# A transformer-and-state-space kernel: its first stage in a new order, with column-grouped modulation products and uniform filter products

## The chip, the cores and the metric

The kernel runs as one program on one NeuronCore of a Trainium2 chip. The metric is the device time of one execution in microseconds (us). The kernel before has a median of 1732.91 us over three runs. The change touches the first stage alone, roughly the first 116 us of the span.

## The reference, cut to what matters

Two blocks follow each other on a sequence of 512 tokens of width 1024, all in float32: an attention layer with a second sequence (`ctx`, 256 tokens) as further keys, a long-convolution ("hyena") layer, two convolutional feed-forwards, then a state-space block. Three pieces of it are computed in the first stage:

```
mod_x = silu(c) @ mod_w[0] + mod_b[0]        # 1024 -> 6*1024; the same for c_ctx
sh1, sc1, ... = split(mod_x, 6)
hx = rmsnorm(x, g) * (1 + sc1) + sh1         # and hc for ctx
kv = hx @ w_dkv                              # first product of the attention layer

# filters of the hyena layer, which need no activations at all
h = sin(freq1 * (z @ w1 + b1)); h = sin(freq2 * (h @ w2 + b2))
h_fwd, h_bwd = split(h @ w3) * exp(-t * |decay|)
filt_f = rfft(concat(h_fwd, 0, reversed h_bwd))
```

## The kernel before, in words

Accurate products of float32 data are made from two rounded parts: `split` writes `hi` (ScalarE) and `lo = x - hi` (VectorE), and `mm3` adds hi*hi, hi*lo and lo*hi. A `Stream` does this for weight blocks of 128x1024: a DMA into a `raw` tile (3 buffers), the `hi` on ScalarE, the `lo` on VectorE (5 buffers each). A float32 product that is not split takes two records on TensorE.

The first stage is written out by hand as a string of tokens, `PLAN`, which `token` works off in order:

- `L` loads and `m` multiplies one of 16 blocks of the modulation weight (128 rows by 1024 columns: 512 of shift, 512 of scale). Blocks 0 to 7 are multiplied in float32 with a stationary operand of 2 columns (`c`, `c_ctx`), blocks 8 to 15 are split first and multiplied with 4 columns. `O` copies the sums out (`scr`), `c` turns them into columns with small products against an identity (`pst`).
- `X` and `C` load tiles of `x` and `ctx`; `q`, `Q` square them and add up; `S`, `T` sum over partitions on TensorE and take 1/rms; `R`, `U` spread that over the partitions on TensorE again; `n`, `N` multiply; `d`, `D` modulate and split.
- `W` loads the three blocks of `w_dkv`; `p` adds one k-step of the three products `psx`, which end the stage's main line.
- `F` advances the generator `hyena_filter` by one `yield`: two steps of the small sine network (`psf`), then for 4 column quarters and 2 signs a `source` (8 products `psh` of 256 columns, then a multiply by the decay window into `ta`), each followed by the `spectrum` of the source before it (16 records `pac`), which is evacuated (`sb`, `ho`) and written to DRAM (`Hd`). `spectrum` has two parts, `q` = 0 and 2, each with its own bank, copy, two adds of 128x256, DMA of 256 KB and `yield`.
- In a `source`, each pair of products uses a stationary tile of 128 rows (`S` whole) and then one of 64 rows (`S[0:64]`).

TensorE's instructions keep the order of the program text (`manual_schedule`). The order on each other queue, SP's list of DMAs among them, is settled at build time by a scheduler with its own idea of when operands are ready, so an entry that it holds to be ready can move ahead of one that stands earlier in the text. Each queue then runs strictly in that order. After the stage come `QPLAN` (four `dq` products, the products of `ctx`) and the attention.

Of the kernel before, what the change touches and what calls it, by code (L numbers as in the profile page):

```python
# [18 lines left out]
L = 512  # L19
# [170 lines left out]
STEPS = "s0 q0 t0 k0 t1 s1 o0 t2 o1 t3 o2 t4 M0 s2 o3 v0 t5 k1 v1 s3 M1 v2 x0 o4 o5"  # L190
PLAN = """F L0 X0 L1 L2 m0 F m1 L3 I9 m2 X1 L4 X6 C4 X3 X7 X4 C0 F X5 X2 q0 L5 V q3 C1 q7 m3 C3 F C5 F m4 L6 L7 q4 L8 q5 q6 L9 m5 F q1 q2 C6 C2 L10 C7 S F R F m6 m7 n3 n0 L11 n6 F n5 L12 n1 O0 m8 m9 F n7 F c0 L13 m10 d1 m11 n2 d0 F L14 F L15 n4 d3 Q0 m12 Q5 F Q7 m13 Q2 m14 m15 d2 O1 F K W0 W1 Q1 c1 W2 d4 F p0 Q4 Q3 F p2 F d7 Q6 T p3 U N0 p1 d5 d6 N3 p6 N7 N1 N2 N6 F p5 N4 D4 D3 D6 N5 p4 F D7 D2 D1 p7 D0 D5 F"""


def build(nc, tc, A, dbg=None):
# [203 lines left out]

    c4 = const.tile([128, 8, 4], F32R, name="c4")
    c2v = c2.rearrange("p (k s) -> p k s", s=2)  # L400
    act.activation(c4[:, :, 0:2], c2v, AF.Copy)
    dve.tensor_tensor(out=c4[:, :, 2:4], in0=c2v, in1=c4[:, :, 0:2].bitcast(F32), op=ALU.subtract)
# [11 lines left out]

    pp = opool(es_a, "pp0", 5, space=PSUM)
    psm = [pp.tile([4, 512], F32, name=f"psm{i}", tag="mm") for i in range(4)]

    def hyena_inputs(hp, t, n1):
        for n, sh, src in (("zT", [33, L], A["zT"]), ("fw1", [33, 64], A["fw1"]), ("fw2", [64, 64], A["fw2"]),
                           ("fv", [64, 4], A["fvec"]), ("fw3", [128, 2048], A["fw3"]), ("nt", [128, 4], A["negt"]),  # L420
                           ("db", [1, 1024], A["dbias"]), ("dec", [128, 1024], A["decay"].broadcast_to([128, 1024])),
                           ("tabs", [128, 1536], A["fwt"]))[len(t):n1]:
            t[n] = hp.tile(sh, F32, name=n)
            nc.sync.dma_start(out=t[n], in_=src)

    def range_sin(tp, out, a, shape, quarter=False, tag=""):

        n = tp.tile(shape, F32, name="rsn" + tag, tag="rsn" + tag if tag else "ho", **({"bufs": 1} if tag else {}))
        if quarter:
# [11 lines left out]
        dve.tensor_scalar(out=r, in0=r, scalar1=PI32, scalar2=-PI32, op0=ALU.min, op1=ALU.max)  # L441
        act.activation(out, r, AF.Sin)

    Hd = dram.tile([2, 8, 128, 512], F32, name="Hd")

    def hyena_filter(hp, tp, pp, t):
        fv = t["fv"]
        src, wgt = t["zT"], t["fw1"]
        for i in range(2):
            ps = pp.tile([128, L], F32, name="psf", tag="mm")  # L450
            pe.matmul(ps[:64], wgt, src, start=True, stop=True)
            a = tp.tile([64, L], F32, name="fa", tag="ho")
# [20 lines left out]
        for i, op in enumerate((ALU.add, ALU.subtract)):  # L473
            w = fw3[:, :1024] if i else hp.tile([128, 1024], F32, name="w3")
            dve.tensor_tensor(out=w, in0=fw3[:, :1024], in1=fw3[:, 1024:], op=op)
            wh = hp.tile([128, 1024], F32R, name=f"w3h{i}", tag=("w3h", "w3")[i])
            wl = hp.tile([64, 1024], F32R, name=f"w3l{i}")
            act.activation(wh, w, AF.Copy)
            dve.tensor_tensor(out=wl, in0=w[0:64], in1=wh[0:64].bitcast(F32), op=ALU.subtract)
            w3.append((wh, wl))  # L480
        W = 256

        def source(qd, ab, win):
            cs = slice(qd * W, qd * W + W)
            ta = []
            for r in range(0, 4, 2):
                ps = pp.tile([128, 2, W], F32, name="psh", tag="mm")
                for e in range(2):
                    pe.matmul(ps[:, e], S[:, r + e], w3[ab][0][:, cs], start=True, stop=False)
                    pe.matmul(ps[:, e], S[0:64, r + e], w3[ab][1][:, cs], start=False, stop=True)  # L490
                a = tp.tile([128, 2, W], F32, name="ta", bufs=4)
                dve.tensor_tensor(out=a, in0=ps, in1=win[:, r:r + 2], op=ALU.mult)
                if r == 0:
                    dve.tensor_copy(a[0:1, 0], db[:, cs])
                ta += [a[:, 0], a[:, 1]]
# [6 lines left out]
        def spectrum(qd, m, ta):  # L502
            s = 1 - m

            for q, (t0, t1), ops in (
                (0, ([(4 * m, 0), (4 * m + 2, 2)], [(4 * m + 1, 1), (4 * m + 3, 3)]), (ALU.add, ALU.subtract)),
                (2, ([(4 * m, 0), (8 + 2 * m, 2)], [(4 * s + 1, 1), (9 + 2 * s, 3)]),
                 (ALU.add, ALU.subtract) if m == 0 else (ALU.subtract, ALU.add)),
            ):
# [8 lines left out]
                f = slice(2 * q + m, 2 * q + m + 3, 2)  # L518
                nc.sync.dma_start(out=Hd[qd // 2, f, :, (qd % 2) * W:(qd % 2) * W + W].rearrange("e p w -> p e w"), in_=o)
                yield  # L520

# [23 lines left out]
    NF = 8  # L545
    mraw = {}
    modw = Stream(A["mod0"], "mod", ahead=0)

    def mod_load(n0, n1):
        for n in range(n0, n1):  # L550
            if n < NF:
                mraw[n] = wp.tile([128, 1024], F32, name="rmod", tag=("whi", "wlo")[n // 4])
                nc.sync.dma_start(out=mraw[n], in_=A["mod0"][n])
            else:
                modw.load(n)

    def mod_mm(n0, n1):
        for n in range(n0, n1):
            k = n % 8
            for i in range(2):  # L560
                if n < NF:
                    pe.matmul(psm[2 * (n // 8) + i][0:2], c2[:, 2 * k:2 * k + 2], mraw[n][:, i * 512:(i + 1) * 512],
                              start=(k == 0), stop=(k == 7))
                for j, w in enumerate(modw.block(n) if n >= NF else ()):
                    pe.matmul(psm[2 * (n // 8) + i], c4[:, k], w[:, i * 512:(i + 1) * 512],
                              start=(k == 0 and j == 0), stop=(k == 7 and j == 1))

    scc = const.tile([128, 16], F32, name="scc")

    def mod_out(hf):  # L570
        nr = 2 if 8 * hf < NF else 4
        scr = [tp.tile([128, L], F32, name="scr", tag="zf", bufs=2)[0:nr] for _ in range(2)]
        act.activation(scr[0], psm[2 * hf][0:nr], AF.Copy)
        dve.tensor_copy(scr[1], psm[2 * hf + 1][0:nr])
        return nr, scr

    def mod_cols(hf, nr, scr):
# [4 lines left out]
        pv = pst.rearrange("p (j n s) -> p j s n", j=2, s=2)  # L582
        o = slice(4 * hf, 4 * hf + 4)
# [77 lines left out]
    def token(t, *i):  # L661
# [6 lines left out]
        elif t == "m":  # L668
            mod_mm(i[0], i[0] + 1)
        elif t == "X":  # L670
# [1264 lines left out]
```

## Time and profile before

| | before |
|---|---|
| runs | 1728.30, 1732.91, 1737.00 us |
| profiled execution | 1726.78 us, span 1725.0 us |
| TensorE busy in the span | 1698.1 us (98%) |
| VectorE / ScalarE busy | 1222.6 us (71%) / 839.8 us (49%) |
| mean granted TensorE clock | 0.992 |

TensorE is busy nearly all the time, though its records overlap, so that a record's length is longer than the distance from one start to the next; in the first stage the distances count. "PEclk" is the granted clock as a share of 2.4 GHz.

### The profile page before, as it was taken

Reading aid. Unit: us, or ns where it says so; the run is one execution under the profiler, and the core shown is the slowest. Engines: PE = TensorE matmul, PEld = TensorE weight load, DVE = VectorE, ACT = ScalarE, POOL = GpSimd, SP = SyncE. Lnnn points to the kernel's source line nnn. Section 1 sums busy time; section 2 is a strip of 40 time slices with the busy share of each in tenths; the row PEclk is TensorE's granted clock in tenths of the full one; section 3 lists DMA queues with packets and bytes.
Section 4 is the critical chain, followed back from the end, with each engine's and each line's share of the span. In section 5 each row is a group of like instructions: output and inputs, shape, how many; then the busy total and the mean of one; then the engine's idle time right before and its main releaser. Section 6 shows DMA issues by size and latency. Waiting matters only on the chain.

```text
span 1725.0 us, 22561 instructions
## 1 busy us (share of the span) xinstructions
PE 1698.1 (98%) x8645; PEld 1409.9 (82%) x8645; DVE 1222.6 (71%) x2065; ACT 839.8 (49%) x1299; POOL 0.7 (0%) x9
## 2 busy tenths in 40 slices
PE   7999999999999999999999999999999999999998
PEld 2688888887988888889888898888888897888887
DVE  5767999885799865654899979884586453927443
ACT  4666989984643314433533355442244244355233
POOL 0000000000000000000000000000000000000000
PEclk8999999999999999999999999999999999999999
DMA  6634332012578772223333332444543347443321
GB/s 241 205 116 150 114 122 86 13 56 69 163 257 268 260 246 95 93 95 98 111 98 98 113 115 74 153 134 148 146 147 98 98 159 155 158 110 121 98 86 49
DMA packets 91862, 224.87 MB, mean 130 GB/s; under 512 B 22728, under 2 KB 38344, under 8 KB 91626
## 3 DMA queue, kind: packets, MB, share of 16 engines
q1 hardware_dynamic: 91754, 223.42, 40.9%
q8 instruction: 68, 1.11, 0.3%
q14 instruction: 40, 0.33, 0.1%
HBM read 206.64 MB, written 16.74 MB: 130 GB/s over the span
## 4 chain that ended last, share of the span: by engine, by line
PE 90%; DVE 5%; ACT 2%; DMA 1%; issue 1%; SPq 0%; DVEq 0%
PE ps_r L264 7%; PE ps_r L265 7%; PE ps_r L266 7%; PE psg L266 5%; PE psg L264 4%; PE psg L265 4%; PE psa L266 4%; PE psa L265 4%; PE psa L264 4%; PE psp L264 3%; PE psp L265 3%; PE psp L266 3%; PE pst L882 2%; PE pac L500 2%; PE pso L893 1%
## 5 line engine op out<-in xcount | busy, mean ns | idle before, releaser
L245 ACT ACTIVATE h_up<-r_up 128x1024 fp32r<-128x1024 f32 x88 | 92.9, 1057 | 149.3 <-PE psg L265 83.1
L264 PE MATMUL ps_r<-mh,h_dn 128*128 128x512 f32 (+1 forms) x407 | 148.5, 365 | 0.0
L265 PE MATMUL ps_r<-ml,h_dn 128*128 128x512 f32 (+1 forms) x407 | 148.3, 364 | 0.0
L266 PE MATMUL ps_r<-mh,l_dn 128*128 128x512 f32 (+1 forms) x407 | 148.3, 364 | 0.0
L246 DVE TENSOR_TENSOR l_up<-r_up,h_up 128x1024 fp32r<-128x1024 f32 x88 | 107.3, 1219 | 52.3 <-ACT h_up L245 47.6
L266 PE MATMUL psg<-hh,l_up 128*128 128x512 f32 x336 | 132.9, 396 | 0.0
L265 PE MATMUL psg<-hl,h_up 128*128 128x512 f32 x336 | 131.7, 392 | 0.0
L264 PE MATMUL psg<-hh,h_up 128*128 128x512 f32 x336 | 131.5, 391 | 0.0
L266 PE MATMUL psa<-hh,l_up 128*128 128x512 f32 x320 | 125.9, 394 | 0.0
L265 PE MATMUL psa<-hl,h_up 128*128 128x512 f32 x320 | 124.6, 389 | 0.0
L264 PE MATMUL psa<-hh,h_up 128*128 128x512 f32 x320 | 124.5, 389 | 0.0
L386 DVE CUSTOM_DVE_ANT_0 mr<-mr,cb 128x1024 f32<-128x1024 f32 x80 | 97.0, 1217 | 21.8 <-DMA mr<-modT 21.8
L245 ACT ACTIVATE h_dn<-r_dn 128x1024 fp32r<-128x1024 f32 x44 | 46.5, 1057 | 106.3 <-PE ps_r L265 69.8
L264 PE MATMUL psp<-hh,h_win 128*128 128x512 f32 x232 | 93.0, 401 | 0.0
L265 PE MATMUL psp<-hl,h_win 128*128 128x512 f32 x232 | 90.8, 392 | 0.0
L266 PE MATMUL psp<-hh,l_win 128*128 128x512 f32 x232 | 90.8, 391 | 0.0
L246 DVE TENSOR_TENSOR l_dn<-r_dn,h_dn 128x1024 fp32r<-128x1024 f32 x44 | 53.6, 1220 | 49.7 <-ACT h_dn L245 48.8
L265 PEld LDWEIGHTS ps_r<-ml,h_dn 128*128 128x128 f32 x407 | 76.5, 188 | 13.6
L264 PEld LDWEIGHTS ps_r<-mh,h_dn 128*128 128x128 f32 x407 | 76.5, 188 | 13.6
L266 PEld LDWEIGHTS ps_r<-mh,l_dn 128*128 128x128 f32 x407 | 76.5, 188 | 13.5
L246 DVE TENSOR_TENSOR l_win<-r_win,h_win 128x1024 fp32r<-128x1024 f32 x32 | 39.0, 1223 | 60.8 <-ACT h_win L245 58.1
L1158 ACT ACTIVATE og<-og 128x512 f32<-128x512 f32 x44 | 27.8, 632 | 109.0 <-DVE og L1115 107.2
(663 smaller groups left out, 4562.2 us busy)
## 6 DMA issues: line engine op xcount, KB each, us to landing
r_up<-wup SPq DMA_DIRECT2D x88, 512.0 KB, 3.7
mr<-modT SPq DMA_DIRECT2D x80, 512.0 KB, 4.3
r_dn<-wdn SPq DMA_DIRECT2D x44, 512.0 KB, 3.9
r_win<-win SPq DMA_DIRECT2D x32, 512.0 KB, 3.5
r_hyin<-hyin SPq DMA_DIRECT2D x24, 512.0 KB, 3.3
rmod<-mod SPq DMA_DIRECT2D x8, 512.0 KB, 7.2
x<-xT SPq DMA_DIRECT2D x16, 256.0 KB, 4.8
Hd<-ho SPq DMA_DIRECT2D x16, 256.0 KB, 2.3
```

Source lines behind the costliest of these rows:

```text
L245: act.activation(hi, raw, AF.Copy)
L246: dve.tensor_tensor(out=lo, in0=raw, in1=hi.bitcast(F32), op=ALU.subtract)
L264: pe.matmul(ps, w[0], a[0], start=start, stop=False)
L265: pe.matmul(ps, w[0], a[1], start=False, stop=False)
L266: pe.matmul(ps, w[1], a[0], start=False, stop=stop)
L386: dve.tensor_tensor_reduce(raw, raw, cb, 1.0, 0.0, ALU.mult, ALU.add, mods[:, n:n + 1])
L500: pe.matmul(ps, tabs[:, o * 128:(o + 1) * 128], ta[r], start=(i == 0), stop=(i == len(terms) - 1))
L882: pe.transpose(pst[:, i * 128:(i + 1) * 128], Pt[h, i][:, j * 128:(j + 1) * 128], ident)
L893: pe.matmul(Ot[h], vw, pth, start=(j == 0), stop=False)
L1158: act.activation(og, og, AF.Silu)
```

## The change

`PLAN` is written anew: the filter's big inputs (`I9`) are loaded ahead of the first modulation block; loads come in pairs; `ctx` is loaded late; its normalization (`T`, `U`, `N`, `D`) follows the last `p`, with the last `F` at the very end. The string has 11 `F` where it had 16, as a spectrum now has one `yield`.

The modulation blocks are all multiplied in float32, without a split. The stationary operand is padded with zeros to 32 columns (`c32`), and for a pair of blocks four products go to four groups of 32 output partitions of one bank: even or odd block, shift or scale half. One copy takes a half out, and four small products with a selection matrix sum even and odd and make the columns.

The filter's `lo` weights get 128 rows, so that each product in `source` uses all 128 rows of `S` (this adds a lo*lo part to the sum). Both parts of a spectrum share one copy of 128x512, two adds of 128x512 and one DMA of 512 KB. The bias row comes from four products of 256 columns in four partition groups. PSUM: the stage's pool has 4 banks (was 5), the filter's 4 (was 3).

```diff
-PLAN = """F L0 X0 L1 L2 m0 F m1 L3 I9 m2 X1 L4 X6 C4 X3 X7 X4 C0 F X5 X2 q0 L5 V q3 C1 q7 m3 C3 F C5 F m4 L6 L7 q4 L8 q5 q6 L9 m5 F q1 q2 C6 C2 L10 C7 S F R F m6 m7 n3 n0 L11 n6 F n5 L12 n1 O0 m8 m9 F n7 F c0 L13 m10 d1 m11 n2 d0 F L14 F L15 n4 d3 Q0 m12 Q5 F Q7 m13 Q2 m14 m15 d2 O1 F K W0 W1 Q1 c1 W2 d4 F p0 Q4 Q3 F p2 F d7 Q6 T p3 U N0 p1 d5 d6 N3 p6 N7 N1 N2 N6 F p5 N4 D4 D3 D6 N5 p4 F D7 D2 D1 p7 D0 D5 F"""
+PLAN = """F I9 L0 L1 X0 X1 F m1 L2 L3 V q0 q1 X2 X3 F m3 L4 L5 q2 q3 X4 X5 m5 F L6 L7 q4 q5 X6 X7 m7 F O0 q6 q7 S L8 L9 F R c0 L10 L11 m9 n0 n1 n2 n3 F
+m11 L12 L13 n4 n5 n6 n7 m13 L14 L15 d0 F d1 W0 W1 m15 O1 p0 d2 p1 F W2 c1 C0 C1 d3 p2 K C2 C3 p3 d4 C4 C5 F p4 C6 C7 d5 Q0 Q1 p5 d6 Q2 Q3 p6 d7 Q4 Q5 p7 Q6 Q7 T
+U N0 N1 N2 N3 D0 D1 N4 N5 D2 D3 N6 N7 D4 D5 D6 D7 F"""
...
-    pp = opool(es_a, "pp0", 5, space=PSUM)
-    psm = [pp.tile([4, 512], F32, name=f"psm{i}", tag="mm") for i in range(4)]
+    pp = opool(es_a, "pp0", 4, space=PSUM)
+    psm = [pp.tile([128, 512], F32, name=f"psm{i}", tag="mm") for i in range(2)]
...
-        for hf in range(2):
-            cs = slice(hf * 512, hf * 512 + 512)
-            ps = pp.tile([128, L], F32, name="psr", tag="mm")
-            pe.matmul(ps[0:1], src[:, 0:1], fw3[0:64, cs], start=True, stop=True)
-            dve.tensor_tensor(out=db[:, cs], in0=ps[0:1], in1=db[:, cs], op=ALU.add)
+        ps = pp.tile([128, L], F32, name="psr", tag="mm")
+        for q in range(4):
+            r_ = slice(32 * q, 32 * q + 1)
+            pe.matmul(ps[r_, 0:256], src[:, 0:1], fw3[0:64, 256 * q:256 * q + 256], start=True, stop=True)
+        for q in range(4):
+            r_ = slice(32 * q, 32 * q + 1)
+            dve.tensor_tensor(out=db[r_], in0=ps[r_, 0:256], in1=db[r_], op=ALU.add)
...
-            wl = hp.tile([64, 1024], F32R, name=f"w3l{i}")
+            wl = hp.tile([128, 1024], F32R, name=f"w3l{i}")
...
-                    pe.matmul(ps[:, e], S[0:64, r + e], w3[ab][1][:, cs], start=False, stop=True)
+                    pe.matmul(ps[:, e], S[:, r + e], w3[ab][1][:, cs], start=False, stop=True)
...
-                ps = pp.tile([128, 2, W], F32, name="pac", tag="mm")
-                acc(ps[:, 0], t0, ta)
-                acc(ps[:, 1], t1, ta)
-                sb = tp.tile([128, W], F32, name="sb")
-                act.activation(sb, ps[:, 1], AF.Copy)
-                o = tp.tile([128, 2, W], F32, name="ho")
-                for e in range(2):
-                    dve.tensor_tensor(out=o[:, e], in0=ps[:, 0], in1=sb, op=ops[e])
...
-                yield
+            odd = pp.tile([128, 2, W], F32, name="pac", tag="mm")
+            acc(odd[:, 0], [(4 * m + 1, 1), (4 * m + 3, 3)], ta)
+            acc(odd[:, 1], [(4 * s + 1, 1), (9 + 2 * s, 3)], ta)
+            even = pp.tile([128, 2, W], F32, name="pac", tag="mm")
+            acc(even[:, 0], [(4 * m, 0), (4 * m + 2, 2)], ta)
+            acc(even[:, 1], [(4 * m, 0), (8 + 2 * m, 2)], ta)
+            sb = tp.tile([128, 2, W], F32, name="sb")
+            act.activation(sb, odd, AF.Copy)
+
+            o = tp.tile([128, 4, W], F32, name="hq")
+            dve.tensor_tensor(out=o[:, 0:3 + m:2 + m], in0=even, in1=sb, op=ALU.add)
+            dve.tensor_tensor(out=o[:, 1:4 - m:2 - m], in0=even, in1=sb, op=ALU.subtract)
+            nc.sync.dma_start(out=Hd[qd // 2, m::2, :, (qd % 2) * W:(qd % 2) * W + W].rearrange("e p w -> p e w"), in_=o)
+            yield
...
-    fpp = opool(es_f, "fpp", 3, space=PSUM)
+    fpp = opool(es_f, "fpp", 4, space=PSUM)
...
-            if n < NF:
-                mraw[n] = wp.tile([128, 1024], F32, name="rmod", tag=("whi", "wlo")[n // 4])
-                nc.sync.dma_start(out=mraw[n], in_=A["mod0"][n])
-            else:
-                modw.load(n)
+            tag, kw = homes[n]
+            mraw[n] = wp.tile([128, 1024], F32, name="rmod", tag=tag, **kw)
+            nc.sync.dma_start(out=mraw[n], in_=A["mod0"][n])
...
+        for n in range(n0, n1, 2):
             for i in range(2):
-                if n < NF:
-                    pe.matmul(psm[2 * (n // 8) + i][0:2], c2[:, 2 * k:2 * k + 2], mraw[n][:, i * 512:(i + 1) * 512],
-                              start=(k == 0), stop=(k == 7))
-                for j, w in enumerate(modw.block(n) if n >= NF else ()):
-                    pe.matmul(psm[2 * (n // 8) + i], c4[:, k], w[:, i * 512:(i + 1) * 512],
-                              start=(k == 0 and j == 0), stop=(k == 7 and j == 1))
+                for e in range(2):
+                    k = n % 8 + e
+                    g = 64 * i + 32 * e
+                    pe.matmul(psm[n // 8][g:g + 32], c32[:, k], mraw[n + e][:, i * 512:(i + 1) * 512],
+                              start=(k < 2), stop=(k > 5))
...
-        for n in range(8):
-            pe.matmul(pst[:, 2 * n:2 * n + 2], scr[n // 4][:, (n % 4) * 128:(n % 4 + 1) * 128], sel if nr == 4 else ident[0:2, 0:2], start=True, stop=True)
+        for n in range(4):
+            pe.matmul(pst[:, 4 * n:4 * n + 4], scr[:, n * 128:(n + 1) * 128], sel, start=True, stop=True)
```

`homes` gives the 16 blocks the buffers of the weight streams: five `whi`, five `wlo`, three `raw`, three more `whi`. An `m` token with an odd number multiplies a pair.

## Rows read from the trace of the kernel before

**Rows 1.** The page, part 4: who holds the chain that ended last.
```profile
PE 90%; DVE 5%; ACT 2%; DMA 1%; issue 1%; SPq 0%; DVEq 0%
```
**Rows 2.** Busy time by stretch: length, each engine, clock, DMA share, GB/s.
```profile
0.00:115.70 115.70, 106.55 (x393) 63.73 (x394) 78.94 (x155) 65.56 (x120) 0.48 (x7) 0.93 0.62 205
19.20:30.80 11.60, 11.60 (x18) 3.25 (x18) 6.82 (x9) 6.88 (x12) 0.00 (x0) 0.50 0.74 266
```
**Rows 3.** Timeline of TensorE, first 20 us: start, length, in brackets idle before.
```profile
7.00 3.57 PE L562 MATMUL psm<-rmod,c 128*2 128x512 f32 x4 [1.56 <-DMA rmod<-mod]
10.50 1.07 PE L451 MATMUL psf<-fg,fw 64*64 64x512 f32 x2
11.50 3.60 PE L562 MATMUL psm<-rmod,c 128*2 128x512 f32 x8
19.18 3.57 PE L464 MATMUL psr<-fw,fg 64*1 64x512 f32 x4 [4.08 <-ACT fg L442]
```
**Rows 4.** Chain that ended last, in order of time: start, length, step.
```profile
26.83 3.50 PE psm L562 x4
...
36.75 3.52 PE psm L562 x8
...
52.45 3.52 PE psm L562 x8
...
57.90 1.85 PE psm L565 x8
...
65.71 1.87 PE pst L581 x16
67.58 1.93 PE psm L565 x8
...
75.48 0.92 PE psm L565 x4
...
80.63 2.78 PE psm L565 x12
```
**Rows 5.** Timeline of TensorE: one source's first product, the spectrum behind it.
```profile
40.21 0.38 PE L489 MATMUL psh<-w3h,fS 128*128 128x256 f32 x1
...
42.71 1.99 PE L500 MATMUL pac<-ta,tabs 128*128 128x256 f32 x8
```
**Rows 6.** Timeline of TensorE: second and last of 72 products of 256 columns.
```profile
128.43 0.28 PE L265 MATMUL psc<-cl,h_wdkv 128*128 128x256 f32 x1
...
136.67 0.28 PE L266 MATMUL psc<-ch,l_wdkv 128*128 128x256 f32 x1
```
**Rows 7.** DMA of 0 to 130 us: GB/s in 40 equal slices of 3.25 us.
```profile
GB/s 26 191 307 411 408 403 386 369 159 0 0 131 313 382 152 293 31 161 270 280 274 294 96 120 299 149 139 263 163 0 166 161 162 0 169 156 0 0 161 25
```
**Rows 8.** Timeline of TensorE: the two steps T and U of ctx.
```profile
100.45 0.50 PE L617 MATMUL ps_st<-ones,saf 128*128 128x1 f32 x4
...
102.98 0.62 PE L627 MATMUL ps_st<-ident,sdf 128*128 128x128 f32 x4
```
**Rows 9.** Instruction groups up to 116 us, shapes apart: count, busy, mean ns, idle before.
```profile
L517 DVE TENSOR_TENSOR ho<-pac,sb 128x256 f32<-128x256 f32 x32 | 11.9, 414 | 4.7 <-ACT sb L514 4.5
L492 DVE TENSOR_TENSOR ta<-psh,win 128x512 f32<-128x512 f32 x16 | 10.8, 684 | 9.3 <-PE psh L490 9.3
L246 DVE TENSOR_TENSOR l_mod<-r_mod,h_mod 128x1024 fp32r<-128x1024 f32 x8 | 9.6, 1212 | 0.6 <-ACT h_mod L245 0.6
L573 ACT ACTIVATE scr<-psm 2x512 f32<-2x512 f32 x1 | 0.6, 586 | 1.2 <-PE psm L562 1.2
```
**Rows 10.** Waits of SP's DMA queue up to 130 us: total, times, longest.
```profile
SPq L519 <- DVE ho L517: 20.6, 10, 11.2
```
**Rows 11.** SP's queue: a load ahead of a write that PLAN puts first.
```profile
55.62 0.33 SPq L242 DMA_DIRECT2D r_mod<-mod  x1
...
57.42 0.38 SPq L519 DMA_DIRECT2D Hd<-ho  x1
```
**Rows 12.** Loads of w_dkv, from issue to landing.
```profile
DMA to landing us min/median/max: 4.2/4.3/4.5
```

More of the change, by code (lines that the diff above doesn't have):

```diff
@@ L397, in build @@
     act.activation(c2, c2, AF.Silu)
[L399 to L402, printed above, removed]
     es_a = ExitStack()
     rp = opool(es_a, "rp", 1, side="right")
+    c32 = rp.tile([128, 8, 32], F32, name="c32")
+    nc.gpsimd.memset(c32, 0.0)
+    dve.tensor_copy(c32[:, :, 0:2], c2.rearrange("p (k s) -> p k s", s=2))
     tp = opool(es_a, "tp0", 2, side="right")
@@ L420, in hyena_inputs @@
                            ("fv", [64, 4], A["fvec"]), ("fw3", [128, 2048], A["fw3"]), ("nt", [128, 4], A["negt"]),
-                           ("db", [1, 1024], A["dbias"]), ("dec", [128, 1024], A["decay"].broadcast_to([128, 1024])),
+                           ("db", [128, 256], None), ("dec", [128, 1024], A["decay"].broadcast_to([128, 1024])),
                            ("tabs", [128, 1536], A["fwt"]))[len(t):n1]:
             t[n] = hp.tile(sh, F32, name=n)
-            nc.sync.dma_start(out=t[n], in_=src)
+            if src is None:
+                for q in range(4):
+                    nc.sync.dma_start(out=t[n][32 * q:32 * q + 1], in_=A["dbias"][:, 256 * q:256 * q + 256])
+            else:
+                nc.sync.dma_start(out=t[n], in_=src)
     def range_sin(tp, out, a, shape, quarter=False, tag=""):
-        n = tp.tile(shape, F32, name="rsn" + tag, tag="rsn" + tag if tag else "ho", **({"bufs": 1} if tag else {}))
+        n = tp.tile(shape, F32, name="rsn" + tag, tag="rsn" + tag if tag else "sb", **({"bufs": 1} if tag else {}))
         if quarter:
@@ L441, in range_sin @@
         dve.tensor_scalar(out=r, in0=r, scalar1=PI32, scalar2=-PI32, op0=ALU.min, op1=ALU.max)
-        act.activation(out, r, AF.Sin)
+        act.activation(r if out is None else out, r, AF.Sin)
+        return r
     Hd = dram.tile([2, 8, 128, 512], F32, name="Hd")
@@ L460, in hyena_filter @@
         fw3, db = t["fw3"], t["db"]
[L461 to L465 removed]
+        ps = pp.tile([128, L], F32, name="psr", tag="mm")
+        for q in range(4):
+            r_ = slice(32 * q, 32 * q + 1)
+            pe.matmul(ps[r_, 0:256], src[:, 0:1], fw3[0:64, 256 * q:256 * q + 256], start=True, stop=True)
+        for q in range(4):
+            r_ = slice(32 * q, 32 * q + 1)
+            dve.tensor_tensor(out=db[r_], in0=ps[r_, 0:256], in1=db[r_], op=ALU.add)
         S = hp.tile([128, 4, 128], F32R, name="fS", tag="zT")
@@ L544, in build @@
     filt = hyena_filter(fhp, ftp, fpp, fin_)
-    NF = 8
     mraw = {}
-    modw = Stream(A["mod0"], "mod", ahead=0)
+    homes = [("whi", {})] * 5 + [("wlo", {})] * 5 + [("raw", {"bufs": rawb})] * rawb + [("whi", {})] * 3
     def mod_load(n0, n1):
         for n in range(n0, n1):
-            if n < NF:
-                mraw[n] = wp.tile([128, 1024], F32, name="rmod", tag=("whi", "wlo")[n // 4])
-                nc.sync.dma_start(out=mraw[n], in_=A["mod0"][n])
-            else:
-                modw.load(n)
+            tag, kw = homes[n]
+            mraw[n] = wp.tile([128, 1024], F32, name="rmod", tag=tag, **kw)
+            nc.sync.dma_start(out=mraw[n], in_=A["mod0"][n])
@@ L568, in build @@
     scc = const.tile([128, 16], F32, name="scc")
     def mod_out(hf):
[L571 to L577, printed above, removed]
+        scr = tp.tile([128, L], F32, name="scr", tag="zf", bufs=2)
+        act.activation(scr, psm[hf], AF.Copy)
+        return scr
@@ L579, in mod_cols @@
+    def mod_cols(hf, scr):
         pst = pp.tile([128, 16], F32, name="pst0", tag="mm")
-        for n in range(8):
-            pe.matmul(pst[:, 2 * n:2 * n + 2], scr[n // 4][:, (n % 4) * 128:(n % 4 + 1) * 128], sel if nr == 4 else ident[0:2, 0:2], start=True, stop=True)
-        pv = pst.rearrange("p (j n s) -> p j s n", j=2, s=2)
+        for n in range(4):
+            pe.matmul(pst[:, 4 * n:4 * n + 4], scr[:, n * 128:(n + 1) * 128], sel, start=True, stop=True)
+        pv = pst.rearrange("p (n j s) -> p j s n", j=2, s=2)
@@ L676, in token @@
             nc.sync.dma_start(out=ident, in_=A["ident"])
-            dve.tensor_tensor(out=sel, in0=ident[0:4, 0:2], in1=ident[0:4, 2:4], op=ALU.add)
+            ids = ident.rearrange("p (j e s) -> p e j s", j=2, e=2)[:, :, :, 0:2]
+            dve.tensor_tensor(out=sel.rearrange("p (j s) -> p j s", j=2), in0=ids[:, 0], in1=ids[:, 1], op=ALU.add)
         elif t == "K":
```

25 lines of the change are left out of this document (8 added, 17 removed).

## The prediction

> **What bounds the kernel now.** I read the chain of work that ended last first: 90% of it is TensorE's own work [rows 1], so time taken out of TensorE's order anywhere reaches the end unless another engine gets in its way. The busy time by stretch says how the first stage stands: in 115.7 us TensorE is idle for 115.70 - 106.55 = 9.15 us, VectorE works 78.9 us and ScalarE 65.6 us, DMA moves 205 GB/s [rows 2]. The timeline of the first 20 us places that idle time: 3.5 us at the start, 1.56 us before the first modulation block, 4.08 us until the sine network is ready for `psr` [rows 3]. From 19.18 us TensorE never waits again before 115.7 us. So the stage is TensorE's list of records plus a slow start, in which 11.6 us ran at a granted clock of 0.50, that is 1.2 GHz [rows 2]. The reader should see that the stage is a sum of distances between starts, and that the other engines have room of 37 us (VectorE) and 50 us (ScalarE).
>
> **Filter products of one shape.** In a source the eight `psh` products with alternating stationary tiles of 128 and 64 rows take from 40.21 to 42.71, 0.3125 us each [rows 5]. Products of the same 256 columns, the same rounded type and 128 rows throughout go from 128.43 to 136.67 in 70 steps, 0.118 us each [rows 6]. I read the difference as what alternation costs. There are 64 such products: 20.0 us become 7.5 us, -12.5 us. Bounds: 0, if something else in a source sets the pace, and -12.5; I take the whole, since shape is the only thing in which the two rows differ. The additional lo*lo rows cost nothing, as a product's time goes by its columns. The `lo` weights of 128 rows have the same free size on VectorE as those of 64.
>
> **Modulation products.** Before: 3.57 + 3.60 us at the start [rows 3], then 3.50 + 3.52 + 3.52 us for the rest of the float32 blocks and 1.85 + 1.93 + 0.92 + 2.78 us for the split ones [rows 4], 25.2 us together. After: 32 float32 products of 512 columns, 64 records. A record of this length takes 3.52 / 8 = 0.44 us at full clock and 3.57 / 4 = 0.89 us at half [rows 3, 4]. No row here shows two products in different groups of output partitions, so the cost has two ends. One after another: 64 x 0.44 = 28.2 us. All four of a pair of blocks at once: two records' time, 0.88 us, for each of eight pairs, 7.0 us. In between lies this: a product is two records into the same group, the second must follow the first, and the four products stand in order, so that only the second record of one group runs beside the first of the next. That is five steps of 0.44 us for a pair, 17.6 us for eight. I take this middle value, because it is wrong by about the same amount (10.6 us) to either side, and keep both ends. The first pair meets the slow clock, +2.2 us: 19.8 us, -5.4 us.
>
> **Small products.** `pst` goes from 32 to 16 records; 16 took 1.87 us [rows 4]: -1.9 us. `psr` was four records of 512 columns at half clock, 3.57 us [rows 3]; it becomes eight of 256. Behind the first pair the clock can be up, which makes 8 x 0.22 = 1.8 us: -1.8 us (ends 0 and -3.1).
>
> **The new start.** The filter's inputs now go first. Until the second block has landed about 3.5 MB must move (1 MB of `fw3`, 0.5 of `decay`, 0.75 of tables, two blocks of 0.5, small ones). At the rates of the first slices, 26, 191, 307, 411 and 408 GB/s for 3.25 us each [rows 7], that is at 14.1 us, with a microsecond to signal it at 15.1. TensorE keeps the two sine products (the second at 10.50 us), loses the four records that stood between them, and so waits 3.5 us, 5.1 us and 3.6 us; I add 1.2 us for the first source (sine, split of `S`, weights), which no longer has `psr` at half clock to hide behind. That is 13.4 us of idle time for 9.15 us: +4.2 us. The earlier `fw3` lets the sine chain run without the weight sum in its middle, which is why I don't charge more; ends 0 and +8.
>
> **The end of the stage.** `T` and `U` stood 102.98 - 100.45 = 2.5 us apart, with one `p` between [rows 8]. Now nothing stands between: the root, the reciprocal and a table load lie bare, 2.5 less its own 0.4: +2.1 us. The last spectrum and the first `dq` products then cover the `ctx` tiles. The three blocks of `w_dkv` need the `raw` buffers of blocks 10 to 12, which `m11` and `m13` free; a load lands 4.3 us after its issue [rows 12] and must be split, while `F` and `m15` run. I put +1.0 us for what sticks out.
>
> **Costed at nothing.** Eight blocks less to split take 9.6 us from VectorE, and the larger adds of a spectrum (16 of about 0.68 us, as `ta`, for 32 of 0.41 us) about 0.9 us [rows 9]; neither engine set the stage's pace, so this is only room. One copy of 128x512 (0.59 us as `scr` [rows 9]) for two smaller ones lies behind the next source's products. Fewer, larger writes of `Hd` move the same bytes. Should TensorE's list shrink further than I think, VectorE's remaining 67 us would be the next limit.
>
> **The sum.** -12.5 - 5.4 - 1.9 - 1.8 + 4.2 + 2.1 + 1.0 = -14.3 us. From the profiled execution's own 1726.8 us that is 1712.5 us. The median of the runs shown lies 6.1 us above that execution; with it the forecast is 1732.9 - 14.3 = 1718.6 us. A difference of 0.5%, 8.7 us, is about what can be told from no change.
>
> **Rival 1: the four groups run one after another.** Then the modulation products cost 28.2 + 1.8 us for the first pair at half clock, 30.0 instead of 19.8 us, and the wait for `w_dkv` is covered: -14.3 + 10.2 - 1.0 = -5.1 us, 1727.8 us. For it speaks that every float32 product in the rows follows its neighbour at 0.44 us with no overlap; against it, that these all go to the same output partitions.
>
> **Rival 2: all four groups run at once.** Modulation costs 7.0 + 0.9 us, 11.9 us less than in my sum: -26.2 us. Then the stage would be 89 us long, VectorE's 67 us with its waits comes near, and the `w_dkv` wait grows by about 4 us: -22 us, 1711 us. The Trainium skill, "TensorEngine Tiling (Array Packing)", section "Theoretical Speedup", states this: operands of at most 32 columns allow up to four independent column tiles; by it the modulation term would be 7.0 us. The Trainium skill's "TensorE: Matmul & The Clock Gate", section "The mechanism", adds that products start and end strictly in order, by which the term would be the middle value, 17.6 us, for products made of two records each. No run here shows either.
>
> **Rival 3: loads caught behind the writes of the filter (slower).** SP's queue runs strictly in order, and writes of `Hd` wait for VectorE: ten waits of 20.6 us in total, the longest 11.2 us [rows 10]. In the new `PLAN` the loads for `m7`, `m13` and the first `p` stand behind the `F` that comes just before those products. If the queue keeps that order, TensorE ends a spectrum, then waits for the copy (0.6 us), two adds (1.4 us), the write's issue and the load's (1.0 us with the signals) and the landing (4.3 us [rows 12]), 7.3 us, three times; with 2.2 us of `m11` beside one of them, 20 us: -14.3 + 20 = +6 us, 1739 us. From the second such stall on the gain is gone. Against it: the build moves loads that it holds to be ready ahead of such writes, as a block's load at 55.62 us stands ahead of a write at 57.42 us that `PLAN` puts first [rows 11]; and the new loads have free buffers up to block 12.
>
> **How the numbers follow.** Middle case 0.50, rival 1 0.20, rival 2 0.15, rival 3 0.15. The middle case's own range, with the ends of start and `psr` and a few microseconds between runs, is 1709 to 1728 us. To leave out no more than 2 in 10 the range reaches from below rival 2, 1703 us, to rival 3, 1739 us. Faster by over 0.5%: most of the middle case (0.43), all of rival 2 (0.15), a quarter of rival 1 (0.05): 0.63. Slower: rival 3's worse half and little else: 0.11. Within: 0.26.
>
> **What would show it.** Eight `psh` in about 1 us instead of 2.5 confirm the largest term. The distance from the first of a pair's modulation records to the next other product tells the three cases apart: 0.9, 2.2 or 3.5 us at full clock. The first of them should start near 15 us. Idle time of TensorE before `m7`, `m13` or the first `p` that a load ends, with SP waiting for `Hd`'s adds, is rival 3. Idle time before `U` should be about 2 us. The prediction is wrong if TensorE is idle in the middle of the stage for more than a few microseconds, or if the clock stays at 0.50 past 20 us: each microsecond of records there would cost another.

## The result and the profile after

The kernel after takes 1708.88 us (median of four runs, 1707.16 to 1713.98), the kernel before 1730.61 us in the same rounds (1725.53 to 1737.00): a ratio of 0.9885, 95% interval 0.9851 to 0.9919. The forecast was 1718.6 us in 1703 to 1739 us, faster: the sign and the range hold, and the time is 9.7 us below the forecast. The profiled execution took 1707.16 us, its span 1705.4 us.

Two rows each mark the end of the first stage: the first sum for the query norm (`pj_tr`), to which the expectations below refer, and the first `dq` product (`psq`). Before:

```profile
L918 PE MATMUL pj_tr<-ones,cqa x8: 242/250/353, 153.2 to 154.1; 128*128 128x1 f32 x8
...
L264 PE MATMUL psq<-hh,h_wdq x32: 388/394/483, 115.5 to 148.1; 128*128 128x512 f32 x32
```

After:

```profile
L920 PE MATMUL pj_tr<-ones,cqa x8: 250/250/353, 136.9 to 137.7; 128*128 128x1 f32 x8
...
L266 PE MATMUL psq<-hh,h_wdq x32: 393/394/587, 98.7 to 131.9; 128*128 128x512 f32 x32
```

So 16 to 17 of the 19.6 us between the spans come out of the first stage. The other 3 us arise after 1400 us in code that the change does not touch; that last piece (from the first `pl` on) took between 315.6 and 327.8 us in the profiles of this study, without an order that goes with an edit. Its length goes with a stretch near 1430 to 1456 us in which the granted clock was 0.50, that is 1.2 GHz. Where there is none (e1, e2, e6, e8, e10) the piece takes 315.6 to 317.0 us; with 3.4 us of it 318.3 (after), with 6.8 us 320.1 to 321.8 (before, e3, e9, e11, e12), with 10.2, 13.7 and 20.5 us 321.9, 323.8 and 327.8 (e4, e7, e5). Before and after:

```profile
1447.50:1454.30 6.80, 6.03 (x22) 5.57 (x23) 1.23 (x1) 2.11 (x3) 0.00 (x0) 0.50 0.65 235
...
1431.40:1434.80 3.40, 3.40 (x13) 3.02 (x13) 1.23 (x1) 1.79 (x3) 0.00 (x0) 0.50 0.26 67
```

I therefore judge every kernel below by its stage.

The chain that ended last, and the busy time by stretch, as [rows 1] and [rows 2]:

```profile
PE 88%; DVE 5%; DMA 2%; ACT 2%; issue 1%; SPq 1%; DVEq 0%; ACTq 0%
```

```profile
0.00:98.75 98.75, 75.85 (x381) 54.06 (x381) 66.76 (x125) 56.74 (x96) 0.72 (x8) 0.98 0.64 226
...
19.20:30.80 11.60, 7.06 (x39) 3.42 (x40) 8.85 (x17) 6.81 (x9) 0.00 (x0) 1.00 0.94 362
```

The 1.00 for 19.20 to 30.80 us needs care. The trace of the kernel after has no record of the clock ahead of 28.5 us (before: ahead of 10.5 us), and a row counts a stretch without one as 1.00. The lengths of the records tell that TensorE ran slowly there too: products of 256 columns start 0.21 us apart at 25 us,

```profile
24.95 0.41 PE L497 MATMUL psh<-w3h,fS 128*128 128x256 f32 x1
25.16 0.41 PE L498 MATMUL psh<-w3l,fS 128*128 128x256 f32 x1
```

and 0.12 us apart from 35.7 us on (below). So I count as work at the low rate what TensorE did ahead of the first clock record and in stretches of 0.50. In the stage that is 20.6 us before and 14.7 us after. By my estimate half of it is what the low rate cost, since records there are about twice as long.

TensorE's busy time in the stage fell from 106.55 to 75.85 us, 30.7 us, but the stage got only about 17 us shorter: TensorE is now idle for 98.75 - 75.85 = 22.9 us, where it was 9.15 us. Nearly half of what the records gave came back as waits. Its waits up to 99 us (total, times, longest):

```profile
PE psf L458 <- ACT rsr L448: 8.4, 1, 8.4
PE psr L470 <- ACT rsr L448: 4.3, 1, 4.3
PE psf L458 <- DMA fw<-fw: 3.4, 1, 3.4
PE psx L266 <- ACT h_wdkv L247: 2.1, 1, 2.1
PE ps_st L627 <- DVE sdf L619: 2.1, 1, 2.1
PE psh L497 <- DVE fS L479: 1.2, 1, 1.2
PE psx L268 <- DVE l_wdkv L248: 1.1, 2, 0.5
PE psh L498 <- DVE w3l L487: 0.4, 1, 0.4
```

TensorE's timeline, to be laid beside [rows 3 to 5]:

```profile
13.68 1.96 PE L458 MATMUL psf<-rsr,fw 64*64 64x512 f32 x2 [8.36 <-ACT rsr L448]
15.57 2.29 PE L567 MATMUL psm<-rmod,c 128*32 128x512 f32 x8
22.12 1.03 PE L470 MATMUL psr<-fw,rsr 64*1 64x256 f32 x8 [4.26 <-ACT rsr L448]
...
34.52 1.06 PE L567 MATMUL psm<-rmod,c 128*32 128x512 f32 x8
35.52 0.39 PE L497 MATMUL psh<-w3h,fS 128*128 128x256 f32 x1
35.74 0.28 PE L498 MATMUL psh<-w3l,fS 128*128 128x256 f32 x1
...
36.45 0.28 PE L498 MATMUL psh<-w3l,fS 128*128 128x256 f32 x1
36.57 3.62 PE L508 MATMUL pac<-ta,tabs 128*128 128x256 f32 x16
```

Eight `psh` take 36.57 - 35.52 = 1.05 us, 0.118 us from start to start behind the first, for 2.50 us [rows 5]. A pair of modulation blocks, eight records, takes 35.52 - 34.52 = 1.00 us; one such block pair took 3.52 us before [rows 4]. The same stretch, records of `psm` alone, shows how:

```profile
34.50:34.60 0.10, 0.08 (x4) 0.08 (x8) 0.00 (x0) 1.00 0.00 0
34.60:34.90 0.30, 0.30 (x4) 0.08 (x8) 0.00 (x0) 1.00 0.00 0
34.90:35.05 0.15, 0.15 (x8) 0.00 (x0) 0.00 (x0) 1.00 0.00 0
```

In the first tenth of a microsecond four records run at once, and the second four join them at about 34.96 us. All eight lie within 1.06 us, though each is about 0.6 us long.

### The profile page after: what moved, and what is told of

It reads as the page before. It is cut to its first block, busy times and chain, and to the rows that moved or that the text cites. A ratio compares the mean times of both kernels' runs of the same rounds, so it can differ in the third digit from the quotient of the medians.

```text
span 1705.4 us, 22478 instructions
## 1 busy us (share of the span) xinstructions
PE 1666.6 (98%) x8633; PEld 1399.5 (82%) x8633; DVE 1211.7 (71%) x2041; ACT 834.4 (49%) x1285; POOL 1.0 (0%) x10
## 3 DMA queue, kind: packets, MB, share of 16 engines
q1 hardware_dynamic: 91632, 223.42, 40.8%
## 4 chain that ended last, share of the span: by engine, by line
PE 88%; DVE 5%; DMA 2%; ACT 2%; issue 1%; SPq 1%; DVEq 0%; ACTq 0%
PE ps_r L266 7%; PE ps_r L268 7%; PE ps_r L267 7%; PE psg L268 5%; PE psg L266 4%; PE psg L267 4%; PE psa L268 4%; PE psa L267 4%; PE psa L266 4%; PE psp L266 3%; PE psp L267 3%; PE psp L268 3%; PE pst L884 2%; PE pac L508 1%; PE pso L895 1%
## 5 line engine op out<-in xcount | busy, mean ns | idle before, releaser
L268 PEld LDWEIGHTS ps_r<-mh,l_dn 128*128 128x128 f32 x407 | 76.5, 188 | 13.6 <-DVE l_dn L248 0.2
L266 PEld LDWEIGHTS ps_r<-mh,h_dn 128*128 128x128 f32 x407 | 76.5, 188 | 13.4
```

What stands on the lines that cost most here:

```text
L266: pe.matmul(ps, w[0], a[0], start=start, stop=False)
L268: pe.matmul(ps, w[1], a[0], start=False, stop=stop)
```

## The experiments

Two theories stood at the start. A: the gain is records taken out of TensorE's list, and the parts add up. B: the new order makes the gain. A single table holds the outcome, all from one profiled execution each; "idle" is the stage (up to `psq`) less TensorE's busy time in it, and "low" is the part of the busy time at the low rate, counted as above.

| kernel | stage | busy | low | idle | `pj_tr` |
|---|---|---|---|---|---|
| before | 115.5 | 106.4 | 20.6 | 9.2 | 153.2 |
| after | 98.7 | 75.8 | 14.7 | 22.9 | 136.9 |
| before + one shape (e5 / e11) | 99.3 / 99.6 | 90.6 / 91.6 | 10.6 / 13.6 | 8.7 / 8.0 | 137.0 / 137.3 |
| before + grouped modulation (e9) | 111.7 | 94.1 | 27.2 | 17.6 | 149.5 |
| after, one group (e1) | 119.4 | 98.8 | 16.6 | 20.6 | 157.7 |
| after, 64-row `lo` weights (e2) | 114.0 | 93.0 | 26.4 | 21.0 | 152.2 |
| after, evacuation in two parts (e3) | 97.8 | 76.3 | 14.4 | 21.5 | 136.2 |
| after, old order (e4) | 103.4 | 77.0 | 19.5 | 26.4 | 141.3 |
| after, weight sums behind the sines (e7) | 101.2 | 78.5 | 19.4 | 22.7 | 139.2 |
| after, weights covered (e6) | 90.9 | 73.1 | 10.7 | 17.8 | 128.9 |
| e6 + sum between the sines (e8) | 90.4 | 74.8 | 13.0 | 15.6 | 128.4 |
| e8 + a block pair ahead (e10) | 89.6 | 76.6 | 15.4 | 13.0 | 127.8 |
| after again (e12) | 100.2 | 77.1 | 17.2 | 23.1 | 138.2 |

After against itself (136.9 and 138.2 in `pj_tr`) shows how far one profile can be trusted: about a microsecond. The clock is enough to explain it: half of 17.2 - 14.7 us is 1.25 us.

**Parts undone in the kernel after.** One column group for the float32 products, with as many banks as that needs; the copies and the 32 small products `pst` of before come back with it (e1):

```diff
-                    pe.matmul(psm[n // 8][g:g + 32], c32[:, k], mraw[n + e][:, i * 512:(i + 1) * 512],
+                    pe.matmul(psm[2 * (n // 8) + i][0:2], c2[:, 2 * k:2 * k + 2], mraw[n + e][:, i * 512:(i + 1) * 512],
...
```

> The changed kernel with the modulation products in one group of output partitions: float32, not split, stationary operand of 2 columns, four banks, new order kept. Theory A (the stage is TensorE's list of records; four groups run at once): 64 records at 0.44 us, 28.2 us for 10.0 us, less the waits that this covers (4.3 us before psr, 3.2 us at the first p and the slow clock behind them): pj_tr starts 9 to 13 us later than the changed kernel's 136.9 us, at 146 to 150 us. Theory B (the new order of loads made the gain, products count little): at most 3 us later, 140 us.

Measured: 1726.53 us, `pj_tr` 157.7 us, 20.8 us later and beyond both ranges. TensorE's busy time in the stage rose by 23.0 us, and the waits gave back only 2.3. Of the 20.8 us about 1 us goes with the clock and 2 us with `pst`; the grouping is worth the rest, some 18 us, in the new order.

The `lo` weights with 64 rows again (e2):

```diff
-            wl = hp.tile([128, 1024], F32R, name=f"w3l{i}")
+            wl = hp.tile([64, 1024], F32R, name=f"w3l{i}")
...
-                    pe.matmul(ps[:, e], S[:, r + e], w3[ab][1][:, cs], start=False, stop=True)
+                    pe.matmul(ps[:, e], S[0:64, r + e], w3[ab][1][:, cs], start=False, stop=True)
```

> The changed kernel with the filter's lo weights and their stationary tile back at 64 rows. Theory A: eight psh take 2.5 us instead of 0.95, 64 of them 12.4 us more, of which the waits at the first p can hide at most one source's share; pj_tr 10 to 13 us later than 136.9 us, at 147 to 150 us. Theory B (order made the gain): under 3 us later.

Measured: 1722.13 us, `pj_tr` 152.2 us, 15.3 us later, again more than expected. Work at the low rate grew from 14.7 to 26.4 us, so some 5.9 us of that goes with the clock and 9.4 us are left, just short of the range. In the source that starts at 42.88 us the eight products start 0.31 us apart, as before:

```profile
42.88 0.39 PE L497 MATMUL psh<-w3h,fS 128*128 128x256 f32 x1
43.19 0.38 PE L498 MATMUL psh<-w3l,fS 64*128 64x256 f32 x1
43.50 0.38 PE L497 MATMUL psh<-w3h,fS 128*128 128x256 f32 x1
...
45.38 2.86 PE L508 MATMUL pac<-ta,tabs 128*128 128x256 f32 x12
```

In the source before it, at the low rate, they were 0.51 us apart. The alternation itself is the price, the same from 128 rows to 64 and back: 0.3125 - 0.118 = 0.19 us for each product. The loads of the stationary tiles (PEld) show where it arises, in the kernel after and in e2:

```profile
35.63 0.19 PEld L498 LDWEIGHTS psh<-w3l,fS 128*128 128x128 f32 x1
35.75 0.19 PEld L497 LDWEIGHTS psh<-w3h,fS 128*128 128x128 f32 x1
...
43.19 0.18 PEld L498 LDWEIGHTS psh<-w3l,fS 64*128 64x128 f32 x1
43.50 0.19 PEld L497 LDWEIGHTS psh<-w3h,fS 128*128 128x128 f32 x1
```

With one shape a load starts 0.11 us ahead of its product (35.63 for the product at 35.74), beside the product before it. With alternating shapes it starts only with its own product (43.19), and its length, 0.18 to 0.19 us, equals the price. The Trainium skill, "TensorEngine Tiling (Array Packing)", section "Key Properties", says that a change of the tiling mode makes TensorE drain. The trace agrees in so far as nothing overlaps at each change of shape; that this is the drain that the page means is not shown.

A spectrum evacuated in two parts (e3):

```diff
-            act.activation(sb, odd, AF.Copy)
-            o = tp.tile([128, 4, W], F32, name="hq")
...
+                act.activation(sb, ps[:, 1], AF.Copy)
+                o = tp.tile([128, 2, W], F32, name="hq", tag="hq")
```

> The changed kernel with a spectrum evacuated in two parts (two copies of 128x256, four adds of 128x256, two writes of 256 KB), still one yield. Theory A: no record of TensorE changes and ScalarE and VectorE have room, so pj_tr stays within 1 us of 136.9 us. Rival (VectorE or SP's queue is near the path): 2 to 5 us later, by 16 issues of writes and 2.2 us more of adds.

Measured: 1709.75 us, `pj_tr` 136.2 us. It costs and gives nothing that one profile can tell, as forecast.

The `PLAN` of before in the kernel after, all else kept (e4):

> The changed kernel with the PLAN of before; products, groups and evacuation stay new. Theory A: the records' sum is the new one and the waits are again near the 9 us of before instead of 22.9 us, so pj_tr starts at 124 to 137 us, and the ratio to before is 0.983 to 0.991. Theory B: the gain goes with the order, pj_tr near 150 us, ratio 0.997 to 1.003.

Measured in three rounds: 1711.54 us, ratio to before 0.9911, interval 0.9883 to 0.9938; `pj_tr` 141.3 us. The records are gone as in the kernel after (77.0 us busy), but 26.4 us are idle, 7.3 of them before `pst`, for the copy `scr`, and 7.3 before `psr`. The order is worth 4.4 us here, some 2.4 us of it by the clock, and not the gain: theory B falls. Theory A's range of 124 to 137 us is missed too, as the waits did not come back to 9 us. The old string holds 21 `F` (not 16, as stated above), and the new generator has work for only 11: the filter's products end before 70 us, and none is left to cover the wait for `scr`. So e4 is not the old order in every respect.

**One part alone in the kernel before.** The diff of e2 the other way round (e5, and the same kernel timed as e11):

> The kernel before with the filter's lo weights at 128 rows and nothing else. Theory A: TensorE never waits in that stage after 19 us, so the whole 12 to 13 us come through: pj_tr at 140 to 142 us for 153.2 us. Theory B: under 3 us earlier; a rival between them (blocks of the modulation weight, their splits or w_dkv are then late): 5 to 9 us earlier.

> The kernel before with 128 rows for the lo weights and nothing else, timed. If one shape makes the whole gain and the new order with the grouped modulation adds nothing, the ratio to the kernel before is that of the kernel after within 0.3% (0.986 to 0.991). If the rest of the change brings a gain in the end that the stage's first sums don't show, it is above 0.992.

Measured: e5 1718.71 us and `pj_tr` 137.0 us, 16.2 us earlier, more than expected. Timed beside the kernel after (e12) on the same chip, before 1728.71 us:

> The kernel after, timed on the same chip in the same rounds as the others: ratio to the kernel before 0.985 to 0.992 as measured already, the query norm's first sum at 136.4 to 137.4 us.

e11 takes 1710.22 us, ratio 0.9902, interval 0.9876 to 0.9929; e12 1707.57 us, ratio 0.9887, interval 0.9864 to 0.9909, as forecast, with `pj_tr` at 138.2 us a little outside its range. The two agree within their intervals. This one part of the change, three lines, makes all of the gain that can be told. In e11 the stage reads:

```profile
0.00:99.60 99.60, 91.57 (x393) 58.54 (x394) 78.12 (x155) 65.13 (x120) 0.48 (x7) 0.97 0.71 238
```

Sources at full clock there take about 1.0 us instead of 2.5, some 12 us for eight. The rest of its 15.9 us goes with the clock: 13.6 us of work at the low rate instead of 20.6, half of which is 3.5 us and leaves 12.4 us. The mean clock of whole runs points the same way, 0.987 to 0.994 in the eleven runs before and 0.991 to 0.997 in the six of e11. Why the clock fell where it did is not shown: from 20 to 31 us it was 1.00 in e5 and 0.75 in e11, which are the same kernel.

The grouped modulation alone (e9; float32 without a split, `c32`, four groups, one copy, four small products):

```diff
-                    pe.matmul(psm[2 * (n // 8) + i][0:2], c2[:, 2 * k:2 * k + 2], mraw[n][:, i * 512:(i + 1) * 512],
+                    pe.matmul(psm[n // 8][g:g + 32], c32[:, k], mraw[n + e][:, i * 512:(i + 1) * 512],
...
```

> The kernel before with the modulation products of the change alone (float32, four groups, pairs of blocks, buffers of the change); order, filter and evacuation stay old. One buffer less for the sine network's output makes room. Theory A: 25.2 us of records become 8 to 10 us and pst halves, so pj_tr is 15 to 18 us earlier than 153.2 us, at 135 to 138 us, if no load is late. Rival (loads or small products become the bound): 8 to 12 us earlier. Theory B: under 3 us earlier.

Measured: 1726.42 us, `pj_tr` 149.5 us, only 3.7 us earlier, below theory A and its rival and just above theory B. TensorE's busy time fell by 12.2 us and its idle time rose by 8.4:

```profile
PE psr L463 <- ACT fg L441: 8.2, 1, 8.2
PE psf L450 <- ACT fg L441: 5.1, 1, 5.1
PE psf L450 <- DMA fw<-fw: 3.4, 1, 3.4
```

This is where theory A's sum fails. Before, the modulation blocks at the start covered the sine chain [rows 3]; made short, they uncover it. The start also stays slow longer: the first clock record comes at 40.8 us instead of 10.5, and 27.2 instead of 20.6 us of work are at the low rate. That is 3.3 us, so the records themselves shrank by some 15.5 us.

**What the idle time hangs on.** The weight sums on VectorE held behind both sine chains (e7):

```diff
-            dve.tensor_tensor(out=w, in0=fw3[:, :1024], in1=fw3[:, 1024:], op=op)
+            tc.keep_in_program_order(dve.tensor_tensor(out=w, in0=fw3[:, :1024], in1=fw3[:, 1024:], op=op))
```

> The changed kernel with the two weight sums of the filter kept in program order on VectorE, so behind the sine chain. Theory A (the second sine product came at 13.68 us instead of 10.50 because VectorE waited for fw3 and did a weight sum and a weight split inside the chain): the second psf at 10.0 to 10.8 us, psr 3 us earlier than 22.1 us, and of that 1 to 3 us at pj_tr, 134 to 136 us. Rival (the next thing on the path, weights w3 or blocks 2 to 5, is as late): psf early, pj_tr unchanged within 0.5 us.

Measured: 1716.48 us, `pj_tr` 139.2 us, 2.3 us later. The wait for the second sine product fell from 8.4 to 5.1 us, and the first source then waited 6.0 us for the weights. The wait was moved, not removed: the idle time is 22.7 us for 22.9. The 2.3 us go with the clock (19.4 instead of 14.7 us at the low rate) and say nothing against the edit.

The order around `w_dkv` and `T` (e6): one step of the filter, `W2` and `c1` go ahead of `p0`, `T` ahead of `p7`:

```diff
-m15 O1 p0 d2 p1 F W2 c1 C0
+m15 O1 F W2 c1 p0 d2 p1 C0
...
-p6 d7 Q4 Q5 p7 Q6 Q7 T
+p6 d7 Q4 Q5 Q6 Q7 T p7
```

> The changed kernel with two moves in PLAN: the F that stood behind p1 goes ahead of p0, with W2 and c1, and T goes ahead of p7. Theory A: the waits for w_dkv (2.1 + 1.1 us), the slow clock behind them (about 1.5 us) and the bare wait before U (2.1 us) go: pj_tr 4 to 7 us earlier than 136.9 us, at 130 to 133 us. Rival (the waits only move to the next load or to ctx): less than 2 us, 135 to 137 us.

Measured in three rounds: 1703.35 us, ratio 0.9871, interval 0.983 to 0.9911; `pj_tr` 128.9 us, 8.0 us earlier, a little more than expected; 5.1 us of it are idle time, and some 2.0 us go with the clock. Both waits for `w_dkv` and the one before `U` are gone, and so is the slow stretch behind them: in the kernel after TensorE ran its first steps of `p` like this,

```profile
60.69 0.39 PE L268 MATMUL psx<-hh,l_wdkv 128*128 128x512 f32 x1
63.20 0.50 PE L266 MATMUL psx<-hh,h_wdkv 128*128 128x512 f32 x1 [2.12 <-ACT h_wdkv L247]
...
67.56 0.63 PE L268 MATMUL psx<-hh,l_wdkv 128*128 128x512 f32 x1
67.99 0.63 PE L266 MATMUL psx<-hh,h_wdkv 128*128 128x512 f32 x1
```

0.43 us apart from 66.7 to 69.3 us, where 0.23 us is normal; the mean granted clock of 60 to 71 us was 0.84, and 1.00 in e6.

In e6, the first weight sum held between the two sine chains, the split of `S` and the sum's remainder right behind the second (e8):

```diff
+            if i:
+                w0 = hp.tile([128, 1024], F32, name="w3")
+                tc.keep_in_program_order(dve.tensor_tensor(out=w0, in0=t["fw3"][:, :1024], in1=t["fw3"][:, 1024:], op=ALU.add))
             a = tp.tile([64, L], F32, name="fa", tag="sb")
...
```

> The kernel after with the two moves of the weights' run (F, W2 and c1 ahead of p0, T ahead of p7), and in the filter network the first weight sum held between the two sine chains on VectorE, with the split of S and of that sum held right behind the second chain and the four additions to db after them. Theory: the 10.50 us of the prediction for the second sine product failed because the weight sum and its remainder stood inside the first sine chain; held between the chains they let it start at 10.4 to 10.8 us (13.70 us with the two moves alone), psr at 18.8 to 19.5 (22.14), the first psh at 22 to 23.2 (24.39), and the query norm's first sum at 126.5 to 128.0 us (128.9). Rival: the sine chain is not what the stage's start hangs on; the first modulation pair or the first psh then waits for a load or for ScalarE's table load, and the norm's first sum stays within 0.5 us of 128.9.

And with the second pair of blocks ahead of the step with `psr` (e10):

```diff
-X2 X3 F m3 L4
+X2 X3 m3 F L4
```

> The same, and the second pair of modulation blocks (m3) ahead of the step with psr, so that its records cover what is left of the second sine chain. Theory: with all four column groups at once a pair is 1.0 us of work at full clock and 2 at half, so the wait before psr falls by 1 to 2 us and the query norm's first sum comes at 125.0 to 127.0 us. Rival: blocks 2 and 3 have not landed before psr can start; then TensorE waits for the transfer ahead of psr and the norm's sum comes no earlier than in the kernel without this move, or up to 3 us later.

Measured in five rounds, before 1728.71 us: e8 1698.71 us, ratio 0.9834, interval 0.9808 to 0.9861, `pj_tr` 128.4 us; e10 1698.36 us, ratio 0.9826, interval 0.9801 to 0.9852, `pj_tr` 127.8 us. The second sine product of e8 starts at 10.47 us and `psr` at 18.91, both as its theory had them, and so is the first `psh`, at 22.73 us. Still the end moved by 0.5 us, as its rival had it: the idle time fell by 2.2 us, but 2.3 us more work fell to the low rate, and the first pair took 3.15 us for 2.29. The waits of e8:

```profile
PE psf L458 <- ACT rsr L448: 5.1, 1, 5.1
PE psf L458 <- DMA fw<-fw: 3.5, 1, 3.5
PE psm L573 <- DMA rmod<-mod: 3.1, 1, 3.1
PE psh L503 <- DVE fS L479: 2.8, 1, 2.8
```

The first pair of blocks has landed at about 15.5 us, and the first source needs the split of `S`, which starts at 21.62 us behind two of the additions to `db` on VectorE, although the edit meant to put it ahead of them. In e10 the wait for that split is gone, but the pair that covers it took 3.2 us at the low rate, and 3.1 us of waits for blocks stay: 0.6 us earlier in the one profile, short of its theory's range. e8 and e10 are the fastest versions found and cannot be told from each other.

## Why the prediction came out as it did

**Filter products of one shape, -12.5 us: right.** 0.118 us each was the price, and the shape was the cause (e2, e11). What the sum left out is that work at the low rate also shrinks: alone, this part is worth 15.9 us of stage, 12.4 without that.

**Modulation products, -5.4 us: mis-sized.** The step that failed is the middle value of 17.6 us: it let only the second record of one group run beside the first of the next. The pairs measured 2.29 (low rate), 2.89 for two (the first at the low rate), 1.00, 1.00, 1.85 for two and 1.00 us, 10.0 us together, where the sum had 19.8: -15.2 us. That is rival 2's case, whose end was 7.9 us. The Trainium skill, "TensorEngine Tiling (Array Packing)", section "Theoretical Speedup", gives up to four times for operands of at most 32 columns; the trace agrees with 3.52 / 1.00 = 3.5 times. The middle value had leaned on the other page, the Trainium skill's "TensorE: Matmul & The Clock Gate", section "The mechanism", which has products start and end strictly in order. The trace does not say which record belongs to which product, so the rule itself is not refuted; my step from it, that a product's second record keeps the next group waiting, is. e1 shows the other end: in one group the 64 records are 30.4 us of busy time, 10.4 in four.

**Small products, -3.7 us: right within a microsecond.** `psr` took 1.03 us for 3.57, `pst` twice 0.95 for twice 1.9.

**The new start, +4.2 us: mis-sized.** The waits up to the first source sum to 3.4 + 8.4 + 4.3 + 1.2 + 0.4 = 17.7 us where I had 13.4. The step that failed is the sentence that the earlier `fw3` lets the sine chain run without the weight sum in its middle. It did the reverse. VectorE in the kernel after:

```profile
6.65 0.42 DVE L440 TENSOR_SCALAR rsn<-rsn 64x512 f32<-64x512 f32 x1
8.24 1.22 DVE L483 TENSOR_TENSOR w<-fw 128x1024 f32<-128x1024 f32 x1 [1.17 <-DMA fw<-fw]
9.38 0.68 DVE L442 SCALAR_TENSOR_TENSOR rsr<-rsn,fa 64x512 f32<-64x512 f32 x1
10.09 0.68 DVE L443 SCALAR_TENSOR_TENSOR rsr<-rsn,rsr 64x512 f32<-64x512 f32 x1
10.70 1.21 DVE L487 TENSOR_TENSOR w3l<-w,w3h 128x1024 fp32r<-128x1024 f32 x1
```

The sum stands inside the first chain, waits 1.17 us there for `fw3`, and its remainder follows two steps later; the second sine product starts at 13.68 us instead of 10.50. I had worked out when `fw3` lands and not where the queue would place its consumer. But e8 shows that mending this alone gives 0.5 us: the landing of the first pair of blocks is next, forecast at 15.1 us and measured, by the pair's start, at 14.8 to 15.5 us in e7, e8 and e10. The microsecond for the signal in that forecast stands on no row.

**The end of the stage, +2.1 and +1.0 us.** The wait before `U` was 2.1 us, right. The waits for `w_dkv` were 3.2 us, and the records behind them ran at a granted clock of 0.50 (66.1 to 69.5 us), about 1.2 us more. This term was mis-sized for two reasons: the `m` pairs that should have covered the splits had become short (rival 2 had put about 4 us on that), and a wait of that kind had no slow clock behind it in my sum.

With the measured terms the sum is -12.4 - 15.2 - 1.9 - 2.5 + 8.5 + 2.1 + 3.2 + 1.2 = -17.0 us; the stage became 16.8 us shorter. That this lies so close to the forecast's 14.3 us is partly luck: the modulation products gave 9.8 us more than the sum had, and the start and `w_dkv` took 7.7 us back. The clock has no term of its own in either sum. The prediction read one stretch of 11.6 us at 0.50, while 20.6 us of TensorE's work were at the low rate before and 14.7 after; and its sign of being wrong, a slow clock past 20 us, came true in the records up to 28.5 us (its other sign, idle time in the middle of the stage, came to 3.2 us). Two slips move no forecast: by its own rows the first pair at half clock adds 3.5 us to rival 1, not 1.8, which makes 1729.5 us, and 78.9 - 9.6 - 0.9 leaves VectorE 68 us, not 67.

**Rival 3** did not come: SP's queue was held by a write from 23.6 to 36.0 us, but TensorE waited for no load behind one. **The same view that was right for one part hid the other:** "from 19.18 us TensorE never waits again" was read as room for the other engines. It held only for TensorE's old list. Once some 15 us of records at the start and middle were gone, the sine chain and the splits of `w_dkv` set the pace, and the grouping with the new order, 15.8 us of records less than e11, came out 0.9 us of stage ahead of it.

Rival 2's time, 1711 us, is the nearest to the measured one, partly by chance: the start was 4.3 us worse than in its sum, and 3 us came from after 1400 us, where the stretch at 0.50 happened to be 3.4 us long instead of 6.8. What stays open: why TensorE's clock falls where it does, and with it how much of a stage's length a second profile would give again.

## What to carry to other kernels

Where TensorE alternates between stationary tiles of different row counts, pad the smaller one: it was three lines and, by itself, the whole measurable gain. Before a saving on the bound engine is booked, list which chains its records were covering; what is saved above such a chain can come back as a wait (8.4 of 12.2 us in e9), and a reorder then has to start from the new waits (e6 and e10 took 8 and then 1 us out of the stage that way, with no record less). A forecast of when an operand lands must also say where in its consumer's queue the instruction stands that waits for it. And before two single profiles are compared, the work at the low clock in each should be counted: it explains e7's 2.3 us and most of what e12 differs from the kernel after.

## What the runs showed of the hardware

Products with 32 stationary columns in four groups of output partitions ran four at a time: 1.00 us for eight records of 512 float32 columns at full clock, 3.52 us with 2 columns in one group. A change between 64 and 128 stationary rows added 0.19 us to each product of 256 columns, as much as the load of its stationary tile takes, which then started only with the product itself. And short waits can cost more than their length: behind 3.2 us of waits between 60.7 and 66.1 us TensorE ran at a lower granted clock (0.84 over 60 to 71 us; again in e7 and e12), and with the waits gone (e6, e8, e10) it did not. That is no rule: e3 had 1.7 us of such waits and kept 1.00 there, and in the kernel before the clock fell to 0.50 at 89.0 us, while TensorE had not waited since 19.2 us:

```profile
88.90:92.40 3.50, 3.50 (x8) 2.57 (x9) 1.72 (x3) 0.00 (x0) 0.00 (x0) 0.51 0.87 255
```
